# A planner that also schedules the lead-in and searches by replays, and gate rows from split sums, in a one-core DiT layer

## The chip, the cores and the metric

One core of a Trainium2 chip runs the program. The metric is device time in microseconds from start to end of one execution; the time before is the median of three executions on the same chip. The profile is of one further execution. Engines: TensorE (PE, with its weight loads PEld), VectorE (DVE), ScalarE (ACT), GpSimd (POOL), and SyncE (SP), which issues nearly all DMAs.

## The reference

One layer of a diffusion transformer in float32: 256 latent tokens and 256 context tokens of width 2048. The conditioning vector c (and c_ctx for the context) gives six modulation vectors through w_ada; the first two scale and shift the input of a q/k/v projection of width 3072, whose heads go to windowed attention with a sink (A) and to global attention with normalised q and k (B). Then an output projection, a gated residual with layer norm, and a SwiGLU network of hidden width 5632, again with gated residual and layer norm.

```python
sh1, sc1, g1, sh2, sc2, g2 = ada_mods(c, w_ada, b_ada)       # silu(c) @ w_ada + b_ada, split in six
h = modulate(x, sh1, sc1) @ w_in                             # likewise for ctx, with its own mods
x = layer_norm(ALPHA * x + g1 * (heads @ w_out), ln1_g, ln1_b)
u = modulate(x, sh2, sc2)
x = layer_norm(ALPHA * x + g2 * ((silu(u @ w_gate) * (u @ w_up)) @ w_down), ln2_g, ln2_b)
```

## The kernel before, in words

**Products.** A float32 product is three fp32r products (`mm3`, lines 291 to 294): both operands are split into a high half (cast to fp32r on ScalarE) and a low half (the difference, on VectorE), and high x high, low x high and high x low are summed in PSUM. Weights come by DMA as raw tiles of 128 partitions and are split in pieces of 128x1024 (lines 282, 283 and 543, 546).

**The planned part** (to some 400 us) computes the modulation columns, q/k/v, attention and the output projection. The 16 tiles of the contraction of the q/k/v projection are taken in five groups of 1, 1, 2, 4 and 8 (`GROUPS`). For each group, `flow_columns` sums the columns of w_ada for shift and scale on TensorE (line 595), copies the bank (line 629), transposes it by small products with `sel` (line 634) and adds the bias (lines 640, 642). `flow_part` transposes x and ctx (line 699), modulates them and splits the result (lines 710 to 727; a group of one tile goes by line 710 and 712). `flow_blocks` and `flow_block` run the products with six blocks of w_in and empty the accumulators to SBUF (lines 778 to 782): in the first two groups each accumulator receives one triple of products and is then emptied, on VectorE for the second. Then follow attention and `flow_out`. `flow_vector` sums the first gate's columns on VectorE all the while.

**What sets the order.** Each piece of work is a step of `Flow`: an engine, an assumed duration, the steps it comes after, and the buffers it takes and gives back. `forward` simulates a list schedule: whenever an engine is free, it starts the ready step of least rank for which buffers are free. `backward` gives each step the latest start that keeps the end, and these become the ranks of the next round; the best of eight rounds (by its own simulated end) is emitted, and every engine then executes its instructions in that order. Loads are charged by row length (`dma_ns`: 390, 340 or 290 bytes per ns), their landing 2 us later. The begin times per engine say from when the plan may use each.

**The lead-in** is not ordered by the plan: `F.pulls` (at the end of the planned part) takes steps out of the planned order and emits them behind a trigger. The transposes of the first group stand behind the first sum; the casts of the first two w_in pieces and the modulations behind the second addition (the copy of the sums, line 629, therefore before the first cast, line 543); the casts of the third and fourth piece behind accumulators' emptying; the column sums of the second group behind 13 products of the first (`PULL`), those of the third behind four of the second. Warm-up products (`warm`, line 342) stand between the quarters of the second sum and, as steps `WARMS`, behind it.

```python
for _ in range(self.ROUNDS):
    order, last = self.forward()
    if last < end:
        best, end = [(s, s.start, [b.pool for b in s.take]) for s in order], last
    late = self.backward(last)
```

**The rest** (not planned by `Flow`) is w_gate and w_up, then w_down in four column blocks (`down_steps`, `last_steps`). Beside the blocks, VectorE sums the second gate's columns (line 416) in four stretches of 512; `ada_rows` ends each with `rows_from`: one float32 product of a tile of ones with the 128x512 sums (line 426), which sums over the partitions and gives the row to all of them, and a copy to `g2sb` (line 427). The split weights go through four buffers for each half (`HL_BUFS`).

Of the kernel before, what the change touches and what calls it, by code (L numbers as in the profile page):

```python
# [46 lines left out]
WARM = 56  # L47
WARMS = (32, 33, 35, 36, 37, 38)
# [8 lines left out]
PULL = 12  # L57
# [14 lines left out]
class Flow:  # L72
# [8 lines left out]
    ROUNDS = 8  # L81

    def __init__(self, room, begin):
        self.room, self.begin, self.steps, self.at, self.pulls = dict(room), begin, [], 0.0, []
# [96 lines left out]
    def run(self):  # L181
        best, end = None, math.inf
        for _ in range(self.ROUNDS):
            order, last = self.forward()
            if not order:
                break
            if last < end:
                best, end = [(s, s.start, [b.pool for b in s.take]) for s in order], last
# [4 lines left out]
        rooms, then, count, done = {}, {}, {}, set()  # L193
        for s, s.start, pools in best:
            rooms[s] = pools
        for trigger, steps in self.pulls:
            if isinstance(trigger, tuple):
                of, i = trigger
                trigger = [s for s, _, _ in best if s in of][i]
            then.setdefault(trigger, []).extend(steps)  # L200
        held = {s for steps in then.values() for s in steps}

        def emit(s):
            done.add(s)
            for b, b.pool in zip(s.take, rooms[s]):
                pass
            s.fn()
            for n in then.get(s, ()):
                emit(n)

        for s, _, _ in best:
            if s not in held:
                emit(s)
        assert len(done) == len(best), "a pulled step has no trigger"
# [3 lines left out]
def dit_layer(ctx: ExitStack, tc: tile.TileContext, x, c, cx, c_ctx, w_ada, b_ada, w_in, q_norm_g,  # L218
# [125 lines left out]
    wps = Buf("wk")  # L344
    wps.t = wk_bank()[:, :P]
# [114 lines left out]
    def const_tables():  # L460
        nc.gpsimd.tensor_scalar_mul(nsink, sinkb, -1.0)
        for t in range(NT):
            for g, cg, sg in ((gq, cosQ, sinQ), (gk, cosK, sinK)):
# [19 lines left out]
             {"SP": 2100.0, "PE": 3800.0, "ACT": 4300.0, "DVE": 4000.0, "POOL": 4000.0})  # L483
# [12 lines left out]
    F.room["b4"] -= 4  # L496
# [82 lines left out]
    last_load, lead = [], {}  # L579

    def flow_columns(c0, ncol, shift, scale, ats, at):

        width = ncol * P
        n1 = ncol == 1
# [16 lines left out]
        for g in range(ns):  # L601
# [3 lines left out]
            ns1 = nk / 4 * (40 + 1.67 * width)  # L605
            if c0:
# [15 lines left out]
            if g == 0:  # L622
                lead[c0, "both"] = prev
# [19 lines left out]

        a = F.add("ACT", 60 + 0.9 * width, copy, [prev], [sb], [bank])
        b = F.add("PE", 224 * ncol, sums, [a], [ps], [sb])
        adds = [F.add("DVE", 160, lambda i=i: add(i), [b], give=[ps]) for i in range(2)]
        if n1:
            lead[c0, "copy"], lead[c0, "sums"], lead[c0, "adds"] = a, b, adds
# [13 lines left out]
    def flow_part(k0, n, at, each):  # L662
# [5 lines left out]
        def load_x():  # L668
            if k0 == 0:
                return  # L670
# [3 lines left out]
        def load_cx():  # L674
            if k0 == 0:
                cx_room.t = cx0
                return
# [4 lines left out]
        F.at = at + 0.5 * each if k0 else -2.0  # L682
        ns = dma_ns(n * P * SEQ * 4, n * P * 4)
        loads = [F.add("SP", max(ns, 500), load_x), F.add("SP", max(ns, 500), load_cx, take=[cx_room])]
        for s in range(2):
# [3 lines left out]
            for j0 in range(0, n, 2):  # L689
# [13 lines left out]
                def modulate(j, s=s, j0=j0, ps=ps, uf=uf, rooms=rooms):  # L703
# [3 lines left out]
                    if n == 1:  # L707
                        rooms[0].t = b4([P, 4, SEQ], F32R, "uh")
                        rooms[1].t = b4([P, 4, SEQ], F32R, "ul")
                        nc.scalar.activation(rooms[0].t[:, 0, :], ps.t[:, :SEQ], AF.Identity,  # L710
                                             bias=shc[:, k, s : s + 1], scale=scc[:, k, s : s + 1])
                        nc.vector.tensor_scalar(uf.t[:, 0, :], ps.t[:, :SEQ], scc[:, k, s : s + 1], shc[:, k, s : s + 1],
                                                op0=ALU.mult, op1=ALU.add)
                        return
                    nc.scalar.activation(uf.t[:, j, :], ps.t[:, j * SEQ : (j + 1) * SEQ], AF.Identity,
                                         bias=shc[:, k, s : s + 1], scale=scc[:, k, s : s + 1])

                def cast(rooms=rooms, j0=j0, nj=nj, uf=uf):
# [1065 lines left out]
```

## Time and profile before

| what | us |
|---|---|
| median of three executions | 1138.43 (1137.34 to 1139.28) |
| the profiled execution: its own time | 1134.76 |
| its span, first to last instruction | 1133.0 |
| TensorE busy | 1111.8 |
| VectorE busy | 841.2 |
| ScalarE busy | 547.5 |
| GpSimd busy | 39.7 |

The profiled execution's own time holds 1.8 us around the span, and lies 3.67 us under the median. Busy time counts an engine's instructions joined where they overlap; a row's own time is that of the instruction from start to its modelled end, so that products in a row overlap and their starts, not their lengths, tell their pace.

### The profile page before, as it was taken

How to read it: one execution, taken by the hardware profiler on the slowest of the kernel's cores; microseconds unless marked ns; L12 is line 12 of the kernel's file. 1: busy time of each engine (PE TensorE's matmuls, PEld its weight loads, DVE VectorE, ACT ScalarE, POOL GpSimd, SP SyncE). 2: the span in 40 equal slices, each digit the busy share in tenths (PEclk: the TensorE clock that was granted, in tenths of full speed). 3: DMA queues.
4: the chain of work that ended last, by engine and by line, in shares of the span. 5: the costliest groups of instructions: out<-in, count | busy, mean ns of one | idle time of the engine just before them, and what ended most of it. 6: DMA issues, size and time to landing. Idle time of an engine off the chain costs nothing.

```text
span 1133.0 us, 14075 instructions
## 1 busy us (share of the span) xinstructions
PE 1111.8 (98%) x5259; PEld 892.6 (79%) x5259; DVE 841.2 (74%) x1066; ACT 547.5 (48%) x790; POOL 39.7 (4%) x82
## 2 busy tenths in 40 slices
PE   8999999999999999999999999999999999999996
PEld 6666588788887787888888888888888888888884
DVE  4763589999989987877767566767766787676576
ACT  3341464877774365454464444445444344333342
POOL 1000050110100001000000000000000000000000
PEclk9999999999999999999999999999999999999998
DMA  9999999686999689998866766777677889877641
GB/s 306 365 393 396 386 370 370 238 261 200 372 334 391 230 309 343 320 326 307 312 223 217 251 223 224 243 243 255 217 249 243 311 314 328 318 283 245 203 147 74
DMA packets 178317, 321.26 MB, mean 284 GB/s; under 512 B 8732, under 2 KB 43196, under 8 KB 175943
## 3 DMA queue, kind: packets, MB, share of 16 engines
q1 hardware_dynamic: 177528, 320.03, 80.9%
q8 instruction: 41, 0.67, 0.2%
q10 hardware_dynamic: 720, 0.33, 0.1%
q14 instruction: 28, 0.23, 0.1%
HBM read 304.07 MB, written 16.25 MB: 283 GB/s over the span
## 4 chain that ended last, share of the span: by engine, by line
PE 91%; DMA 4%; DVE 2%; ACT 2%; issue 0%; POOL 0%; DVEq 0%; SPq 0%; ACTq 0%; POOLq 0%
PE acc L292 28%; PE acc L294 27%; PE acc L293 27%; PE wk L1025 2%; PE wk L595 2%; DMA raw<-in_w_in_dram 2%; DMA raw<-in_w_ada_dram 1%; DMA pd<-hx 1%; DVE lo L546 1%; PE wk L292 1%; PE wk L294 1%; PE wk L293 1%; DMA raw<-in_w_gate_dram 1%; DVE lo L283 1%; ACT hi L543 0%
## 5 line engine op out<-in xcount | busy, mean ns | idle before, releaser
L283 DVE TENSOR_TENSOR lo<-raw,hi 128x1024 fp32r<-128x1024 f32 x258 | 311.8, 1221 | 173.2 <-ACT hi L282 170.4
L282 ACT CAST hi<-raw 128x1024 fp32r<-128x1024 f32 x258 | 270.6, 1055 | 334.7 <-PE acc L294 296.5
L292 PE MATMUL acc<-hi,u2h 128*128 128x512 f32 x704 | 274.7, 390 | 0.2 <-ACT hi L282 0.2
L293 PE MATMUL acc<-lo,u2h 128*128 128x512 f32 x704 | 274.1, 389 | 0.8 <-DVE lo L283 0.8
L294 PE MATMUL acc<-hi,u2l 128*128 128x512 f32 x704 | 274.0, 389 | 0.0
L293 PEld LDWEIGHTS acc<-lo,u2h 128*128 128x128 f32 x704 | 132.2, 188 | 28.5 <-DVE lo L283 1.1
L292 PEld LDWEIGHTS acc<-hi,u2h 128*128 128x128 f32 x704 | 132.1, 188 | 28.5 <-ACT u2h L1559 0.8
L294 PEld LDWEIGHTS acc<-hi,u2l 128*128 128x128 f32 x704 | 132.1, 188 | 27.9 <-DVE u2l L1560 0.5
L543 ACT CAST hi<-raw 128x1024 fp32r<-128x1024 f32 (+1 forms) x86 | 87.7, 1030 | 107.4 <-DMA raw<-in_w_in_dram 51.3
L292 PE MATMUL acc<-hi,hTh 128*128 128x512 f32 x344 | 135.6, 394 | 0.4 <-ACT acc L1709 0.4
L294 PE MATMUL acc<-hi,hTl 128*128 128x512 f32 x344 | 133.9, 389 | 0.0
L293 PE MATMUL acc<-lo,hTh 128*128 128x512 f32 x344 | 133.9, 389 | 0.0
L416 DVE SCALAR_TENSOR_TENSOR adav<-raw,cs,adav 128x512 f32<-128x512 f32 (+1 forms) x128 | 121.3, 948 | 12.3 <-DMA raw<-in_w_ada_dram 10.3
L546 DVE TENSOR_TENSOR lo<-raw,hi 128x1024 fp32r<-128x1024 f32 (+1 forms) x86 | 101.7, 1193 | 17.3 <-ACT hi L543 17.3
L292 PE MATMUL acc<-hi,uh 128*128 128x512 f32 x256 | 103.1, 403 | 2.6 <-DVE kvacc L782 1.1
L293 PE MATMUL acc<-lo,uh 128*128 128x512 f32 x256 | 100.3, 392 | 2.0 <-DVE lo L546 2.0
L294 PE MATMUL acc<-hi,ul 128*128 128x512 f32 x256 | 100.2, 392 | 0.3 <-DVE ul L727 0.3
L292 PEld LDWEIGHTS acc<-hi,hTh 128*128 128x128 f32 x344 | 64.6, 188 | 15.2 <-issue 1.0
L293 PEld LDWEIGHTS acc<-lo,hTh 128*128 128x128 f32 x344 | 64.6, 188 | 14.3 <-issue 0.7
L294 PEld LDWEIGHTS acc<-hi,hTl 128*128 128x128 f32 x344 | 64.6, 188 | 13.3
L292 PEld LDWEIGHTS acc<-hi,uh 128*128 128x128 f32 x256 | 48.1, 188 | 20.4 <-issue 7.0
L293 PEld LDWEIGHTS acc<-lo,uh 128*128 128x128 f32 x256 | 48.1, 188 | 12.0 <-DVE lo L546 3.0
(219 smaller groups left out, 1137.6 us busy)
## 6 DMA issues: line engine op xcount, KB each, us to landing
raw<-in_w_ada_dram SPq DMA_DIRECT2D x70, 1024.0 KB, 7.0
raw<-in_w_gate_dram SPq DMA_DIRECT2D x44, 1024.0 KB, 5.2
raw<-in_w_up_dram SPq DMA_DIRECT2D x44, 1024.0 KB, 5.1
raw<-in_w_down_dram SPq DMA_DIRECT2D x44, 1024.0 KB, 4.9
raw<-in_w_ada_dram SPq DMA_DIRECT2D x48, 512.0 KB, 5.2
raw<-in_w_in_dram SPq DMA_DIRECT2D x18, 1024.0 KB, 7.0
raw<-in_w_out_dram SPq DMA_DIRECT2D x16, 1024.0 KB, 8.0
pd<-hx SPq DMA_DIRECT2D x64, 128.0 KB, 4.1
```

The source lines that it names most:

```text
L282: nc.scalar.copy(hi[:, :n], raw[:, s : s + n])
L283: nc.vector.tensor_tensor(lo[:, :n], raw[:, s : s + n], hi[:, :n].bitcast(F32), op=ALU.subtract)
L292: nc.tensor.matmul(ps, lhsT=xh, rhs=w[0], start=first, stop=False, skip_group_check=seeded)
L293: nc.tensor.matmul(ps, lhsT=xh, rhs=w[1], start=False, stop=False, skip_group_check=seeded)
L294: nc.tensor.matmul(ps, lhsT=xl, rhs=w[0], start=False, stop=last, skip_group_check=seeded)
L416: nc.vector.scalar_tensor_tensor(a[:, c : c + piece], raw[:, f : f + piece], cs[:, 4 * (g * (G4 * NB // w) + j) + 2, None], a[:, c : c + p ...
L543: nc.scalar.copy(hl.hi[:, :n], raw.t[:, s : s + n])
L546: nc.vector.tensor_tensor(hl.lo[:, :n], raw.t[:, s : s + n], hl.hi[:, :n].bitcast(F32), op=ALU.subtract)
L595: nc.tensor.matmul(bank.t[32 * j : 32 * j + 32, :width], lhsT=cs[:, 4 * k + 2 - 2 * i : 4 * k + 34 - 2 * i], rhs=raw.t[:, c * width : (c + ...
L1025: nc.tensor.matmul(o_ps.t[:, : 2 * P].rearrange("p (g q) -> p g q", q=32), lhsT=v, rhs=pv[:, k], start=k == 0, stop=k == 3)
```

## The change

`Flow.run` no longer moves steps by `pulls`. A new `search` makes eight rounds of `forward` and `backward` with noise on the ranks, then 800 moves, each of which shifts the ranks of a random part of the steps and makes a new forward schedule. A schedule is judged by `replay`: it runs the order through in-order engines with buffers used first in, first out, once by the assumed durations and four times with each duration varied by 3%, and the mean end decides. The lead-in's steps are ordered by this plan like the rest; they have new durations and begin times, the small w_in pieces are charged to the b4 buffers in which they stand, and the first group's transposes come after the first column sum. The `warm` products between quarters are left out; two stand behind the second sum and four behind the small products with `sel`. For the second gate's rows, the sums are split in halves and multiplied by an fp32r tile of ones: a cast on ScalarE, a difference on VectorE and two fp32r products.

```diff
-WARM = 56
-WARMS = (32, 33, 35, 36, 37, 38)
-PULL = 12
...
+    SEED, SIGMA, MOVES, DRAWS, JITTER = 312, 600.0, 800, 4, 0.03
...
+    def replay(self, order, draws):
+
+        index = {s: i for i, s in enumerate(order)}
+        gives, left = {}, {}
...
+        free, plan = {p: [None] * n for p, n in self.room.items()}, []
+        for s in order:
+            deps = [(index[a], self.lag(a, s) - early) for a, early in s.after]
+            for b in s.take:
+                if not free[b.pool]:
+                    return math.inf
+                old = free[b.pool].pop(0)
+                for g in gives.get(old, ()):
+                    deps.append((index[g], self.AGAIN if b.pool.endswith("raw") else self.OTHER[g.eng]))
...
+            plan.append((s.eng, s.ns, deps))
+        total = 0.0
+        for draw in draws:
+            busy, ends = dict(self.begin), []
+            for (eng, ns, deps), f in zip(plan, draw):
+                t = busy[eng]
+                for i, lag in deps:
+                    if ends[i] + lag > t:
+                        t = ends[i] + lag
+                busy[eng] = t + ns * f
+                ends.append(busy[eng])
+            total += max(ends)
+        return total / len(draws)
...
+    def search(self):
+        rng = random.Random(self.SEED)
+        draws = [[1.0] * len(self.steps)]
+        draws += [[max(0.8, rng.gauss(1.0, self.JITTER)) for _ in self.steps] for _ in range(self.DRAWS)]
...
             for i, s in enumerate(self.steps):
-                s.rank = (late[s], i)
+                s.rank = (late[s] + rng.gauss(0.0, sigma), i)
...
+        for _ in range(self.MOVES):
+            sigma, share = rng.choice((100.0, 300.0, 1000.0)), rng.choice((0.01, 0.03, 0.1, 0.3))
+            for r, s in zip(base, self.steps):
+                s.rank = (r[0] + (rng.gauss(0.0, sigma) if rng.random() < share else 0.0),) + r[1:]
...
+            order, last = self.forward()
+            if not order or last > score + 1000:
+                continue
+            mean = self.replay(order, draws)
+            if mean <= score:
+                best, score, base = self.keep(order), mean, ranks
+        return best, score
...
+    def split_rows(sb, dst, s):
+        hi = whl.tile([P, SUB * NB], F32R, tag="hi", name="hi")[:, :NB]
+        lo = whl.tile([P, SUB * NB], F32R, tag="lo", name="lo")[:, :NB]
+        split(hi, lo, sb[:, s : s + NB])
+        ps = wk_bank()
+        nc.tensor.matmul(ps, lhsT=onesr, rhs=hi, start=True, stop=False)
+        nc.tensor.matmul(ps, lhsT=onesr, rhs=lo, start=False, stop=True)
+        nc.scalar.copy(dst[:, s : s + NB], ps)
...
     def ada_rows(c0, dst, sums):
         def done(sb):
             for s in range(0, dst.shape[-1], NB):
-                rows_from(sb, dst, s)()
+                split_rows(sb, dst, s)
...
-             {"SP": 2100.0, "PE": 3800.0, "ACT": 4300.0, "DVE": 4000.0, "POOL": 4000.0})
+             {"SP": 1800.0, "PE": 6300.0, "ACT": 5100.0, "DVE": 4200.0, "POOL": 4000.0})
+    F.room["wk"] -= 1
...
-                prev = F.add("PE", 2 * ns1 + 420, both, [l0, l1, prev], [bank] if g == 0 else [], [r0, r1])
+                prev = F.add("PE", 1860, both, [l0, l1, prev], [bank] if g == 0 else [], [r0, r1])
             else:
-                def quarters(i, r):
-                    for q in range(4):
-                        fn(0, i, r, 4 * q, 4 * q + 4)
-                        if i and 0 < q < 3:
-                            warm(wps.t, 1)
-
-                prev = F.add("PE", ns1, lambda r=r0: quarters(0, r), [l0, prev], [bank] if g == 0 else [], [r0])
-                lead["sum"] = prev
-                prev = F.add("PE", ns1, lambda r=r1: quarters(1, r), [l1, prev], [], [r1])
+                def one(i, r):
+                    fn(0, i, r, 0, nk)
+                    if i:
+                        warm(wps.t, 2)
+
+                prev = F.add("PE", 1080, lambda r=r0: one(0, r), [l0, prev], [bank], [r0])
+                first_sum.append(prev)
+                prev = F.add("PE", 1520, lambda r=r1: one(1, r), [l1, prev], [], [r1])
...
+            if c0 == 0:
+                warm(wps.t, 4)
...
-        loads = [F.add("SP", max(ns, 500), load_x), F.add("SP", max(ns, 500), load_cx, take=[cx_room])]
+        if k0:
+            loads = [F.add("SP", max(ns, 500), load_x), F.add("SP", max(ns, 500), load_cx, take=[cx_room])]
+        else:
+            loads = first_sum * 2
+            cx_room.pool, cx_room.t = "b4", cx0
...
+                if n == 1:
+                    a = F.add("ACT", 520, high, [p] + ready, rooms)
+                    b = F.add("DVE", 470, whole, [a], [uf], [ps])
+                    b = F.add("DVE", 360, rest, [b], give=[uf])
+                    u[k0, s][1].append((a, b))
+                    continue
...
-                piece, = flow_weights(w_in, k0, 1, b0 * NB, m * NB, where, small=k0 == 0)
-                if k0 == 0:
-                    lead["w", i] = piece[1]
+                piece, = flow_weights(w_in, k0, 1, b0 * NB, m * NB, where if k0 else ("b4",), small=k0 == 0)
...
-            v = F.add("PE", 1800, values, g, [o_ps], [pT, *kv_room[w]])
+            v = F.add("PE", 1540, values, g, [o_ps], [pT, *kv_room[w]])
...
-    T = 18.0
+    T = 12.0
...
-    F.pulls.append((lead["sum"], [flip0, flip1]))
-    F.pulls.append((lead[0, "adds"][1], [w0, mod0, l0, rest0, mod1, rest1, w1, l1]))
-    for i in (2, 3):
-        F.pulls.append((lead["evacs"][2 * i - 3], list(lead["w", i])))
...
-    F.pulls.append(((made, PULL), [lead[P, "both"]]))
...
+    onesr = pb.tile([P, P], F32R, tag="onesr", name="onesr")
+    nc.scalar.copy(onesr, ones)
```

## Rows read from the trace of the kernel before

**Rows 1.** The page: the span, and the chain that ended last by engine.
```profile
span 1133.0 us, 14075 instructions
...
PE 91%; DMA 4%; DVE 2%; ACT 2%; issue 0%; POOL 0%; DVEq 0%; SPq 0%; ACTq 0%; POOLq 0%
```

**Rows 2.** By stretch (us): its length, engines busy (instructions), granted clock, DMA share, GB/s.
```profile
0.00:20.00 20.00, 16.62 (x133) 12.72 (x133) 8.85 (x14) 7.13 (x12) 3.48 (x9) 1.00 0.94 291
...
13.29:20.00 6.71, 5.45 (x22) 3.86 (x21) 5.79 (x9) 3.98 (x6) 0.00 (x0) 1.00 1.05 307
20.00:30.00 10.00, 9.50 (x98) 7.42 (x99) 5.63 (x12) 3.35 (x7) 0.00 (x0) 1.00 1.03 335
30.00:43.00 13.00, 11.21 (x92) 6.65 (x92) 10.41 (x17) 3.58 (x6) 0.00 (x0) 1.00 0.97 333
43.00:80.00 37.00, 37.00 (x208) 25.48 (x208) 24.09 (x37) 12.16 (x16) 0.00 (x0) 1.00 1.04 395
80.00:150.00 70.00, 68.67 (x385) 46.64 (x384) 34.93 (x47) 30.06 (x50) 0.00 (x0) 1.00 1.03 387
150.00:300.00 150.00, 150.00 (x696) 122.34 (x695) 140.95 (x237) 102.01 (x219) 27.66 (x54) 1.00 0.84 293
300.00:350.00 50.00, 48.18 (x208) 38.76 (x207) 45.61 (x61) 36.83 (x66) 0.00 (x0) 1.00 1.00 351
350.00:400.00 50.00, 49.90 (x252) 38.92 (x250) 44.43 (x76) 19.02 (x30) 1.60 (x5) 1.00 0.83 305
...
860.00:1100.00 240.00, 240.00 (x1053) 197.27 (x1052) 170.31 (x178) 94.78 (x95) 1.58 (x3) 1.00 0.77 272
...
1100.00:1133.00 33.00, 21.69 (x95) 17.30 (x93) 22.67 (x37) 10.49 (x27) 0.00 (x0) 0.88 0.17 64
```

**Rows 3.** TensorE's waits, 6 to 400 us: total us, times, longest us.
```profile
PE acc L293 <- DVE lo L546: 2.0, 3, 0.8
PE acc L294 <- DVE oTl L1037: 1.8, 1, 1.8
PE acc L292 <- DVE kvacc L782: 1.1, 2, 0.8
PE wk L595 <- DMA raw<-in_w_ada_dram: 0.6, 1, 0.6
```

**Rows 4.** The lead-in in order of time: start us, length us, instruction [idle before it].
```profile
9.95 0.49 PE L342 MATMUL wk<-ident 128*128 128x128 f32 x2
...
11.67 0.27 ACT L629 COPY ada<-wk 128x128 f32<-128x128 f32 x1 [2.19 <-PE wk L595]
11.84 0.62 ACT L543 CAST hi<-raw 128x512 fp32r<-128x512 f32 x1
...
13.29 0.50 PE L292 MATMUL acc<-hi,uh 128*128 128x512 f32 x1
...
13.73 0.68 DVE L546 TENSOR_TENSOR lo<-raw,hi 128x512 fp32r<-128x512 f32 x1
...
14.47 0.51 PE L293 MATMUL acc<-lo,uh 128*128 128x512 f32 x1 [0.67 <-DVE lo L546]
...
25.08 1.95 PE L595 MATMUL wk<-raw,cs 128*32 128x128 f32 x64
```

**Rows 5.** The first gate row of the last stage, in order of time.
```profile
904.31 1.06 ACT L282 CAST hi<-raw 128x1024 fp32r<-128x1024 f32 x1 [3.02 <-PE acc L294]
...
905.25 0.40 PE L294 MATMUL acc<-hi,hTl 128*128 128x512 f32 x1
...
905.48 1.02 PE L426 MATMUL wk<-adav,ones 128*128 128x512 f32 x2
...
906.54 0.59 ACT L427 COPY g2sb<-wk 128x512 f32<-128x512 f32 x1 [1.17 <-PE wk L426]
...
906.58 0.39 PE L293 MATMUL acc<-lo,hTh 128*128 128x512 f32 x1
...
907.02 1.05 ACT L282 CAST hi<-raw 128x1024 fp32r<-128x1024 f32 x1
```

More of the change, by code (lines that the diff above doesn't have):

```diff
@@ L179, in backward, with keep @@
         return start
-    def run(self):
-        best, end = None, math.inf
+    def replay(self, order, draws):
+        index = {s: i for i, s in enumerate(order)}
+        gives, left = {}, {}
+        for s in order:
+            for b in s.give:
+                gives.setdefault(b, []).append(s)
+                left[b] = left.get(b, 0) + 1
+        free, plan = {p: [None] * n for p, n in self.room.items()}, []
+        for s in order:
+            deps = [(index[a], self.lag(a, s) - early) for a, early in s.after]
[5 more added lines that the diff above has]
+                    deps.append((index[g], self.AGAIN if b.pool.endswith("raw") else self.OTHER[g.eng]))
+            for b in s.give:
+                left[b] -= 1
+                if left[b] == 0:
+                    free[b.pool].append(b)
+            plan.append((s.eng, s.ns, deps))
[11 more added lines that the diff above has]
+        return total / len(draws)
+    def keep(self, order):
+        return [(s, s.start, [b.pool for b in s.take]) for s in order]
+    def search(self):
+        rng = random.Random(self.SEED)
+        draws = [[1.0] * len(self.steps)]
+        draws += [[max(0.8, rng.gauss(1.0, self.JITTER)) for _ in self.steps] for _ in range(self.DRAWS)]
+        best, score, sigma = None, math.inf, self.SIGMA
         for _ in range(self.ROUNDS):
+            ranks = [s.rank for s in self.steps]
             order, last = self.forward()
@@ L186, in run @@
                 break
-            if last < end:
-                best, end = [(s, s.start, [b.pool for b in s.take]) for s in order], last
+            mean = self.replay(order, draws)
+            if mean < score:
+                best, score, base = self.keep(order), mean, ranks
             late = self.backward(last)
             for i, s in enumerate(self.steps):
-                s.rank = (late[s], i)
+                s.rank = (late[s] + rng.gauss(0.0, sigma), i)
+            sigma *= 0.8
         assert best, "no step can start"
[L193 to L205, printed above, removed]
+        for _ in range(self.MOVES):
+            sigma, share = rng.choice((100.0, 300.0, 1000.0)), rng.choice((0.01, 0.03, 0.1, 0.3))
+            for r, s in zip(base, self.steps):
+                s.rank = (r[0] + (rng.gauss(0.0, sigma) if rng.random() < share else 0.0),) + r[1:]
+            ranks = [s.rank for s in self.steps]
+            order, last = self.forward()
+            if not order or last > score + 1000:
+                continue
+            mean = self.replay(order, draws)
+            if mean <= score:
+                best, score, base = self.keep(order), mean, ranks
+        return best, score
+    def run(self):
+        for s, s.start, pools in self.search()[0]:
+            for b, b.pool in zip(s.take, pools):
                 pass
             s.fn()
[L208 to L214, printed above, removed]
 @with_exitstack
@@ L642, in add @@
                 nc.vector.scalar_tensor_tensor(scale, pv[:, :, 1, :], 1.0, bc, op0=ALU.add, op1=ALU.add)
[L644 to L648, printed above, removed]
+        a = F.add("ACT", 60 + 0.82 * width, copy, [prev], [sb], [bank])
+        b = F.add("PE", 217 * ncol - 70 if c0 else 1150, sums, [a], [ps], [sb] if c0 else [sb, wps])
+        adds = [F.add("DVE", 160, lambda i=i: add(i), [(b, 0 if c0 else 1000)], give=[ps]) for i in range(2)]
         return a, adds
@@ L767, in flow_block @@
                                         done + len(cols) == ng, ends.get(r))
-                lead.setdefault(("products", k0), []).append(ends[r])
                 for m in rooms:
@@ L1406, in dit_layer @@
     a = F.add("DVE", 3300, lambda: scalars(0), [(outs[n, 0], 80) for n in range(4)])
-    (flip0, mod0, rest0), (flip1, mod1, rest1) = (lead[0, s] for s in range(2))
-    (w0, l0), (w1, l1) = (lead["w", i] for i in range(2))
-    F.pulls.append((lead["sum"], [flip0, flip1]))
-    F.pulls.append((lead[0, "adds"][1], [w0, mod0, l0, rest0, mod1, rest1, w1, l1]))
-    for i in (2, 3):
-        F.pulls.append((lead["evacs"][2 * i - 3], list(lead["w", i])))
-    (flip0, mod0, rest0), (flip1, mod1, rest1) = (lead[P, s] for s in range(2))
-    made = lead["products", 0]
-    F.pulls.append(((lead["products", 1], 3), [lead[2 * P, "both"]]))
-    F.pulls.append(((made, PULL), [lead[P, "both"]]))
-    F.pulls.append(((made, PULL), [lead[P, "copy"]]))
-    F.pulls.append(((made, PULL + 1), [lead[P, "sums"], *lead[P, "adds"]]))
-    F.pulls.append(((made, PULL + 2), [flip0, flip1, mod0, rest0, mod1, rest1]))
     zroom = [Buf("wk"), Buf("wk")]
```

53 lines of the change are left out of this document (17 added, 36 removed).

## The prediction

> **What bounds the kernel now.** I read the page first: one chain, and 91% of it is TensorE [rows 1]. So time is gained only where TensorE stands still or where its own work shrinks. Next the table by stretch [rows 2], to see where it stands still: from 860 to 1100 us it is busy 240.00 of 240.00, and it is full from 43 to 80 and from 150 to 300. What is left inside the planned part (from the first product at 13.29 us [rows 4] to about 400 us) is 1.26 + 0.50 + 1.79 us between 13.29 and 43, 1.33 between 80 and 150, 1.82 between 300 and 350 and 0.10 after that: 6.8 us. The list of waits [rows 3] says whom TensorE waited for: VectorE nearly always (the low halves of w_in, the emptying of the accumulators, once 1.8 us for oTl), and a load only once, 0.6 us, in the lead-in. The lead-in in order of time [rows 4] shows what one wait costs. L292 starts at 13.29 and L293 at 14.47, 1.18 us later. Products that follow each other start 0.23 us apart (L294 at 905.25, the next at 905.48 [rows 5]). So 0.95 us is lost where the list puts 0.67: a wait costs about 0.28 us more than its idle time, since the matmuls no longer overlap. The waits number seven between 13.29 and 43 us and four after (those of 0.6 us and less in all, but for the load, are not shown): the lead-in loses 3.55 + 7 x 0.28 = 5.5 us, the rest of the plan 3.25 + 4 x 0.28 = 4.4. **Nothing that reorders the plan can return more than 9.9 us.**
>
> **The change, part by part.**
>
> *The search.* It adds no instruction. It gives another order on all five queues up to about 400 us, scored with in-order queues, first-in-first-out buffers and 3% noise on the durations. Its gain lies between the 9.9 us above and a loss that the trace bounds only by its like: the longest wait of TensorE there is 1.8 us, 2.1 with the filling [rows 3], and two new ones of that size would cost 4.2. I take a third of the 9.9. In the lead-in that is 1.8 of 5.5: VectorE is busy 10.41 of 13 us from 30 to 43 and the transfers fill their engines (share 0.94 to 1.05) [rows 2], so order can move work there but make no room. In the rest it is 1.4 of 4.4, most of it from the oTl wait, which is an order on VectorE and no lack of its time. A third and not all, because a plan by average durations has already been followed here and these waits are what was left between plan and chip; the same gap will open elsewhere.
>
> *The lead-in as steps.* The pulls go: transposes after the first sum, the first w_in pieces and modulations after the second addition, the next group's column sums behind 13 products (at 25.08 us [rows 4]). The same instructions are issued, now where the planned start puts them, their loads on SP too. What is new is the order on ScalarE. Before, the copy of the first sums (11.67) comes ahead of the cast of the first w_in piece (11.84, 0.62 us) [rows 4]. The new durations put the landing of that piece at 1.8 + 2 x 3.6 + 0.7 + 2.0 = 11.7 and the end of the second sum at about 12.5, so I expect the cast first. If the piece lands as late as 11.84, the copy and all behind it wait until 12.46: up to 0.8 us later, with the sums on TensorE, the two additions, the modulations and the first product behind them. In exchange the low half (0.68 us on VectorE) can be made before the additions, and the 0.95 us of the second product goes. Ends: 0.8 lost, 0.95 gained; I take nothing, near the middle, and keep 0.9 each way for the range.
>
> *The warm-up products.* Two calls between the quarters of the second sum go, the six after it stay as two and four. The two ran while the next quarter was on its way (0.49 us at 9.95, two records) [rows 4], so they cost nothing and their going returns nothing. The cover is that wait; gone, it would be 2 x 0.2 us gained. A loss would come by the clock: the granted clock is 1.00 (2.4 GHz) in every stretch to 1100 us and 0.88 on average in the last one, after TensorE has stopped [rows 2]. A quarter's eight to sixteen products still run between any two waits, so I put nothing.
>
> *The pools.* The small w_in pieces are now charged to the b4 buffers in which they stand and no longer to raw buffers, so loads may be planned earlier. The transfers are full to 150 us [rows 2]; earlier issue only lengthens the queue. Nothing.
>
> *The last stage's gate rows.* Four times the fp32 product with ones becomes a cast, a subtraction and two fp32r products. Now: L426 starts at 905.48 and the second product after it at 906.58 [rows 5], 1.10 us, of which one product is 0.23; so 0.87. Then: 2 x 0.23 = 0.46. Gain 0.41 x 4 = 1.6 us, on the path, since TensorE has no gap there [rows 2]. Added beside it: on ScalarE 0.62 us and on VectorE 0.68 us, four times (the same shapes in [rows 4]); these engines are busy 95 and 170 of 240 us [rows 2]. The wait that it adds: the two products stand behind cast and subtraction, and these behind the sums on VectorE; behind them on TensorE stands the next step of w_down. The pair of operands also takes one of four buffers, so one later cast starts a half step later. In [rows 5] the cast at 907.02 starts 1.65 us after the one before it has ended (904.31 + 1.06), held up by the copy at 906.54, and TensorE had no wait; that much delay is covered. If the cover is gone it is a wait like that of the first product, 0.95 x 4 = 3.8 us lost. I take the gain: the row says that the cover is there. The copy of ones once: 0.2 us on ScalarE, beside products.
>
> **Sum.** 1.8 + 1.4 + 1.6 = 4.8 us off the profiled execution's own 1134.76 us: 1129.96. That execution was 3.67 us under the median of the three runs (1138.43); against the median it is 1133.6.
>
> **A rule against it.** The transfers moved 395 GB/s from 43 to 80 us [rows 2]. The Trainium skill, DMA: Bandwidth & Descriptors, section Bandwidth, has loads from HBM bound at about 358 GB/s per core; by that the plan's 390 for long rows would be out of reach, its lead-in would starve, and the lead-in's 1.8 us would not be there (sum 3.0). The trace goes past that figure, so I keep the sum; the case itself is weighed as rival B.
>
> **The rivals.**
>
> *A. Most of the waits go.* Two thirds of 9.9 us, plus 1.6: 8.2 off, 1130.2. For it: the waits are those of order on VectorE, which is idle in between. The data would be there: up to group 2's first product the kernel needs w_ada for four rows of tiles (8.4 MB), w_in for two (3.1), x and context (1.0) and a first half megabyte, 13.1 MB; by 43 us it had moved 5.8 + 3.35 + 4.3 = 13.5 [rows 2]. Against it: that leaves nearly no slack. 0.17.
>
> *B. Order gives nothing.* The transfers and VectorE pace the lead-in, and what one wait gives back the next takes. Only the last stage remains: 1.6 off, 1136.8. For it: shares of 0.97 to 1.05 to 43 us [rows 2]. This is also the case in which the change doesn't do what it says. 0.20.
>
> *C. Slower: TensorE waits for loads in the lead-in.* In the queue of TensorE a column sum now stands where the plan expects its data, no longer behind products that were counted by hand. The plan charges 390, 340 or 290 GB/s by row length, some 365 for the mix; from 20 to 43 us the trace moved 335 and 333 [rows 2], 7.7 MB, so a plan by those rates, 21.1 us where the trace took 23.0, is 1.9 us early. Each column sum that is reached so blocks the ready products behind it: 1.9 + 0.28 = 2.2 us, twice (for groups 2 and 3) 4.4, less 1.6: 2.8 slower, 1141.2. It decides once such waits pass the 4.8 us of the sum. Against it: before, TensorE waited for a load only 0.6 us [rows 3]. 0.17.
>
> **The numbers.** About 0.2%, 2.3 us, is what a measurement of this kernel can tell from no change. The forecast, a third of the waits and the last stage, has 0.46, its own range 1131.5 to 1135.8 (the 0.9 us of the order on ScalarE and half of the third either way). With A faster is 0.63, B makes 0.20 for the same, C 0.17 for slower. The range from 1128.5 to 1141 takes in A and most of C.
>
> **What would show it.** Right: between 13 and 43 us under 3 us of idle TensorE; no wait on oTl over 1 us; in the last stage two products of ones 0.23 us apart with no idle before them; the cast at about 11.7 ahead of the copy. Wrong: TensorE waiting for w_ada after 20 us (C); the first product after 14.1 us; a granted clock under 1.00 before 1100 us; a wait of L293 just behind a gate row (the buffer); unchanged idle time up to 400 us (B).

## The result, and the profile after

Beside 20 runs of the kernel before (median 1135.80 us, 1132.21 to 1139.49) the changed kernel took 1140.14 us (20 runs, 1135.29 to 1144.66): a ratio of 1.0034, 95% interval [1.0021, 1.0047]. It is slower by 4.3 us at the medians. The forecast of 1133.6 was set against 1138.43 us; the ratio makes 1142.3 of that, above the upper end of the range (the median of 1140.14 itself lies inside it). The profiled executions are 1134.76 us (span 1133.0) and 1137.55 us (span 1135.8).

The page of the kernel after: its span, and the chain that ended last by engine.

```profile
span 1135.8 us, 14062 instructions
...
PE 93%; DVE 3%; ACT 1%; DMA 1%; issue 0%; ACTq 0%; SPq 0%; DVEq 0%
```

Against [rows 1], 1% of the chain is DMA where 4% was. How far the two kernels have come can be read from one tile after the other. The view by tile, first products of each weight with the high half of an operand (count, shortest, median and longest in ns, then the first and the last start in us); first the kernel before:

```profile
L292 PE MATMUL acc<-hi,uh x256: 387/389/582, 13.3 to 254.1; 128*128 128x512 f32 x128
L292 PE MATMUL acc<-hi,oTh x128: 389/389/792, 254.7 to 387.3; 128*128 128x512 f32 x128
L292 PE MATMUL acc<-hi,u2h x704: 389/389/502, 392.1 to 877.6; 128*128 128x512 f32 x176
L292 PE MATMUL acc<-hi,hTh x344: 389/389/798, 878.3 to 1118.5; 128*128 128x512 f32 x172
```

and the kernel after:

```profile
L331 PE MATMUL acc<-hi,uh x256: 389/389/796, 16.1 to 260.0; 128*128 128x512 f32 x128
L331 PE MATMUL acc<-hi,oTh x128: 389/389/798, 257.9 to 390.0; 128*128 128x512 f32 x128
L331 PE MATMUL acc<-hi,u2h x704: 389/389/501, 396.4 to 882.2; 128*128 128x512 f32 x176
L331 PE MATMUL acc<-hi,hTh x344: 389/389/499, 882.9 to 1121.5; 128*128 128x512 f32 x172
```

The first product is 2.8 us late, the last of the planned part (oTh) 2.7, the first after the handover to the second half (u2h) 4.3, the first of w_down (hTh) 4.6 and its last 3.0. So the last stage gained 1.6 us, as forecast, and of the 4.6 us that the kernel is behind at the first hTh product 4.3 were lost before 400 us. The table by stretch of the kernel after (length, engines busy with their instructions in the order PE, PEld, DVE, ACT, POOL, granted clock, DMA share, GB/s), against [rows 2]:

```profile
10.00:20.00 10.00, 6.08 (x41) 4.05 (x38) 5.83 (x11) 4.32 (x7) 0.00 (x0) 0.79 1.09 356
16.06:22.50 6.44, 5.63 (x12) 3.97 (x13) 4.98 (x9) 1.02 (x2) 0.00 (x0) 0.50 1.08 340
20.00:30.00 10.00, 10.00 (x95) 7.98 (x94) 6.17 (x9) 3.89 (x7) 0.00 (x0) 0.87 0.83 275
30.00:43.00 13.00, 13.00 (x84) 9.80 (x83) 10.16 (x19) 3.44 (x6) 0.00 (x0) 1.00 1.03 367
...
80.00:150.00 70.00, 70.00 (x388) 47.23 (x387) 34.51 (x46) 27.16 (x42) 0.00 (x0) 1.00 1.02 385
...
200.00:300.00 100.00, 96.93 (x449) 76.12 (x447) 92.60 (x181) 76.29 (x182) 14.32 (x38) 1.00 0.78 261
300.00:350.00 50.00, 50.00 (x219) 40.91 (x218) 46.89 (x64) 37.66 (x67) 0.00 (x0) 1.00 0.99 348
350.00:400.00 50.00, 48.62 (x239) 37.82 (x238) 45.15 (x73) 18.40 (x27) 1.08 (x4) 1.00 0.89 329
400.00:440.00 40.00, 38.05 (x184) 31.00 (x183) 35.76 (x49) 24.50 (x38) 2.46 (x5) 1.00 0.82 286
860.00:1100.00 240.00, 240.00 (x1060) 198.61 (x1059) 174.02 (x185) 98.66 (x101) 1.58 (x3) 1.00 0.78 276
```

and three stretches of the kernel before that [rows 2] do not have:

```profile
10.00:20.00 10.00, 8.73 (x59) 6.36 (x55) 6.03 (x11) 5.38 (x9) 0.00 (x0) 1.00 1.04 335
...
200.00:300.00 100.00, 100.00 (x475) 80.94 (x474) 94.08 (x186) 78.89 (x189) 13.38 (x38) 1.00 0.77 253
400.00:440.00 40.00, 39.07 (x181) 31.70 (x182) 35.98 (x44) 22.99 (x32) 3.80 (x5) 1.00 0.84 302
```

The search did what it was made for where it could see: the 0.50 + 1.79 + 1.33 us of idle TensorE between 20 and 150 us are gone, and so are the 1.82 between 300 and 350. But TensorE now stands still for 3.92 us from 10 to 20 (1.27 before), 3.07 from 200 to 300 (none before), 1.38 from 350 to 400 (0.10) and 1.95 from 400 to 440 (0.93). And from the first product to 22.5 us it ran at a granted clock of 0.50 (1.2 GHz): the 5.63 us that it was busy there are work of some 2.8 us at full speed (an estimate: half of them). Its waits, 6 to 400 us, against [rows 3]:

```profile
PE wk L679 <- ACT ada L674: 1.4, 1, 1.4
PE acc L331 <- ACT u2h L1580: 1.4, 1, 1.4
PE wk L644 <- DMA raw<-in_w_ada_dram: 1.3, 3, 0.6
PE acc L333 <- DVE oTl L1080: 1.1, 2, 0.6
PE acc L332 <- DVE lo L596: 1.0, 1, 1.0
PE acc L331 <- ACT uh L757: 1.0, 1, 1.0
PE acc L333 <- DVE ul L772: 0.8, 1, 0.8
```

and one more at 402.7 us, from the same view of 400 to 460 us:

```profile
PE wk L1432 <- DVE xt L1215: 1.9, 1, 1.9
```

The oTl wait of 1.8 us is down to 0.6. New are a chain by ScalarE (ada, uh) and VectorE (ul) in the lead-in, and two waits at the handover (u2h, xt). The lead-in in order of time, against [rows 4]:

```profile
11.20 0.43 PE L644 MATMUL wk<-raw,cs 128*32 128x128 f32 x8 [0.32 <-DMA raw<-in_w_ada_dram]
11.56 0.71 PE L381 MATMUL wk<-ident 128*128 128x128 f32 x4
12.39 1.04 ACT L593 CAST hi<-raw 128x1024 fp32r<-128x1024 f32 x1 [2.86 <-DMA raw<-in_w_in_dram]
13.34 0.26 ACT L674 COPY ada<-wk 128x128 f32<-128x128 f32 x1
...
13.50 0.62 ACT L593 CAST hi<-raw 128x512 fp32r<-128x512 f32 x1
13.66 0.39 PE L679 MATMUL wk<-sel,ada 128*128 128x4 f32 x2 [1.39 <-ACT ada L674]
13.90 1.14 PE L381 MATMUL wk<-ident 128*128 128x128 f32 x8
14.49 1.05 ACT L593 CAST hi<-raw 128x1024 fp32r<-128x1024 f32 x1 [0.38 <-DMA raw<-in_w_in_dram]
...
15.45 1.02 ACT L757 ACTIVATE uh<-wk,shc,scc 128x256 fp32r<-128x256 f32 x2
16.06 0.80 PE L331 MATMUL acc<-hi,uh 128*128 128x512 f32 x1 [1.02 <-ACT uh L757]
```

The first sums end at 11.63, but ScalarE has stood 2.86 us in front of the cast of a w_in piece that lands at 12.39; the copy of the sums queues behind it (13.34; before 11.67), and two more casts stand ahead of the modulation (15.45).

### The profile page after: what moved, and what is told of

The parts are those of the page before. It is cut to its first block, busy times and chain, and to the rows that moved or that the text cites. A ratio compares the mean times of both kernels' runs of the same rounds, so it can differ in the third digit from the quotient of the medians.

```text
span 1135.8 us, 14062 instructions
## 1 busy us (share of the span) xinstructions
PE 1112.2 (98%) x5255; PEld 893.2 (79%) x5255; DVE 844.4 (74%) x1070; ACT 551.4 (49%) x795; POOL 41.6 (4%) x82
## 4 chain that ended last, share of the span: by engine, by line
PE 93%; DVE 3%; ACT 1%; DMA 1%; issue 0%; ACTq 0%; SPq 0%; DVEq 0%
PE acc L331 28%; PE acc L333 28%; PE acc L332 28%; PE wk L644 2%; PE wk L1068 2%; PE wk L743 1%; PE wk L331 1%; DVE hx L1050 1%; PE wk L333 1%; PE wk L332 1%; DMA raw<-in_w_in_dram 1%; DMA cxt<-in_ctx_dram 0%; DVE lo L596 0%; PE wk L1401 0%; PE wk L475 0%
## 5 line engine op out<-in xcount | busy, mean ns | idle before, releaser
L333 PEld LDWEIGHTS acc<-hi,ul 128*128 128x128 f32 x256 | 48.6, 190 | 12.3 <-DVE ul L772 1.7
```

What stands on the lines that cost most here:

```text
L333: nc.tensor.matmul(ps, lhsT=xl, rhs=w[0], start=False, stop=last, skip_group_check=seeded)
```

## The experiments

Eleven kernels ran, each beside the kernel before. The clock is the mean over the executions of a kernel of the granted TensorE clock that each run lists (to three places); time x clock is the mean of the products, an estimate of what the kernel would take had the clock always been full. The estimate is rough: the last stretch, at 0.88 over 33 us in [rows 2] with TensorE busy for 21.69 of them, lowers every mean, and warm_more, which has the plan of after, comes out 1.7 us above after. The row of before belongs to the runs beside rows_only, lead_order, warm_more and flips_first; beside the others the median of before was 1135.43 to 1135.80, and each ratio is taken against its own.

| kernel | us, median (runs) | ratio to before, 95% | clock | time x clock |
|---|---|---|---|---|
| before | 1134.99 (35) | 1 | 0.9964 | 1131.4 |
| after | 1140.14 (20) | 1.0034 [1.0021, 1.0047] | 0.9922 | 1130.9 |
| rows_only | 1132.93 (12) | 0.9977 [0.9961, 0.9993] | 0.9968 | 1129.6 |
| lead_order | 1138.63 (12) | 1.0023 [1.0006, 1.0040] | 0.9942 | 1131.8 |
| warm_more | 1137.58 (12) | 1.0019 [1.0004, 1.0034] | 0.9954 | 1132.6 |
| flips_first | 1137.04 (12) | 1.0019 [1.0004, 1.0033] | 0.9933 | 1130.0 |
| both | 1135.63 (12) | 1.0001 [0.9989, 1.0013] | 0.9954 | 1130.5 |
| both_late | 1134.96 (12) | 0.9991 [0.9980, 1.0003] | 0.9963 | 1130.7 |
| values_1800 | 1135.44 (12) | 0.9999 [0.9986, 1.0011] | 0.9938 | 1128.4 |
| seed_4 | 1143.49 (6) | 1.0064 [1.0047, 1.0082] | 0.9917 | 1133.6 |
| val_lead | 1133.10 (12) | 0.9980 [0.9970, 0.9990] | 0.9968 | 1129.6 |
| val_sum2 | 1134.04 (12) | 0.9987 [0.9971, 1.0003] | 0.9955 | 1129.1 |
| val_sum2_warm | 1131.10 (6) | 0.9960 [0.9946, 0.9973] | 0.9973 | 1128.3 |

**rows_only**, the kernel before with the gate rows alone:

```
-                rows_from(sb, dst, s)()
+                split_rows(sb, dst, s)
+    onesr = pb.tile([P, P], F32R, tag="onesr", name="onesr")
+    nc.scalar.copy(onesr, ones)
```

> The kernel before with the split gate rows of the last stage alone; its plan and lead-in are untouched. Theory 1 (the parts are independent): 0.4 us for each of four rows, 1.6 us faster than before, ratio about 0.9986, and no wait of TensorE on either product of ones. Rival (the split takes a buffer that the next casts need): a wait of L293 behind a row, up to 0.95 us each, ratio 1.000 to 1.002.

0.9977, faster than both kernels. The first product of each of its four rows, in the view by tile, and then the first row in order of time in the kernel after:

```profile
L428 PE MATMUL wk<-hi,onesr x4: 389/389/389, 905.1 to 1053.5; 128*128 128x512 f32 x4
```

```profile
904.18 0.69 DVE L328 TENSOR_TENSOR lo<-adav,hi 128x512 fp32r<-128x512 f32 x1 [1.56 <-ACT hi L327]
...
910.08 0.39 PE L468 MATMUL wk<-hi,onesr 128*128 128x512 f32 x1
910.31 0.39 PE L469 MATMUL wk<-lo,onesr 128*128 128x512 f32 x1
```

The two products start 0.23 us apart and find their operands 5 us old: the added cast and subtraction are covered. This part of the change is right and worth the 0.2% alone; the loss is in the rest.

**lead_order**, the plan of after with the lead-in's instructions issued in the order of before (copy, sums and additions, narrow cast, modulations; the wide cast after them), and the two first small loads of w_in changed over:

```
-        for s, s.start, pools in self.search()[0]:
+        for s, s.start, pools in lead_order(self.search()[0]):
...
+    chunk = [copy, sums, *adds, c1, h0, w0, r1, u0, h1, w1, u1, c0, r0]
```

> The changed kernel; the same plan, but in the lead-in the copy of the first sums, the additions and the modulations are emitted ahead of the casts of all but one small w_in piece, and the two first small loads change places, as in the kernel before. Theory 1 (what the lead-in loses stays lost, since TensorE is full from 20 to 200 us): first product at 13.3 us instead of 16.1, granted clock 1.00 throughout, 3 to 4 us faster than the changed kernel, ratio to before 1.000 to 1.001. Rival (the loads set the pace to 150 us): first product early as well, but TensorE waits for loads or for VectorE before 100 us and the end moves by under 1 us, ratio 1.003.

```profile
11.65 0.27 ACT L674 COPY ada<-wk 128x128 f32<-128x128 f32 x1 [2.16 <-PE wk L644]
...
12.65 1.02 ACT L757 ACTIVATE uh<-wk,shc,scc 128x256 fp32r<-128x256 f32 x2 [0.22 <-DVE shc L687]
...
13.27 0.49 PE L331 MATMUL acc<-hi,uh 128*128 128x512 f32 x1
```

With the same warming products the first product comes at 13.27: the 2.8 us are the order of the lead-in. How much of it is ScalarE's order, and how much that of the two loads and of VectorE, which changed with it, this run does not separate. The granted clock was 1.00 from 10 to 30 us. Yet the ratio fell only to 1.0023. In the profiled execution the clock fell elsewhere, at the handover:

```profile
400.00:410.00 10.00, 8.77 (x31) 7.32 (x32) 6.24 (x13) 3.85 (x8) 0.95 (x1) 0.66 0.42 146
```

**warm_more**, after with more warming products in the lead-in's waits and the order untouched:

```
-                        warm(wps.t, 2)
+                        warm(wps.t, 9)
...
-                warm(wps.t, 4)
+                warm(wps.t, 10)
```

> The changed kernel with 9 in place of 2 warm-up products behind the second sum and 10 in place of 4 behind the small products; the plan and every other order are the same. Theory 1 (the granted clock fell because TensorE had little to do from 11.5 to 16 us): the clock stays at 1.00, the first product stays at 16.1 us, the products from 16 to 22.7 us follow each other 0.23 us apart instead of 0.43, up to 3 us are gained by 25 us and about 2 at the end, ratio 1.0015. Rival (VectorE, which empties one accumulator per product there, or the loads hold the pace at either clock): clock 1.00, but waits of TensorE between 17 and 33 us take the gain back, ratio 1.003.

The first product stays late (15.88 us in the profiled execution), but the clock does not fall in the lead-in; it fell once in the attention:

```profile
10.00:20.00 10.00, 8.42 (x68) 7.11 (x69) 5.78 (x11) 4.31 (x7) 0.00 (x0) 1.00 1.09 358
...
235.00:245.00 10.00, 8.98 (x35) 6.70 (x36) 8.56 (x16) 6.46 (x24) 0.00 (x0) 0.83 0.70 234
```

The mean clock went from 0.9922 to 0.9954 and the median 2.6 us down (by the ratios 0.0015, 1.7 us; the two intervals overlap). So the clock costs time of its own, apart from the order.

**flips_first**, after with the transposes of the second half (L1432) ahead of the column sums (L1401) on TensorE, as before had them; **both**, this and lead_order; **both_late**, both with the scale sums merged one step later, so that they stand no longer inside the second layer-norm chain on VectorE:

```
-    run(merge(first_half[3 : 2 * ONE_F], scales))
+    run(first_half[3:4])
+    run(merge(first_half[4 : 2 * ONE_F], scales))
```

> The changed kernel; the same plan, but the two transposes for the next stage (L1432) are emitted on TensorE ahead of the column sums of L1401, as they stood before, and nothing else moves. Theory 1 (the handover loses because the chain from the transposes over ScalarE and VectorE to the next products is no longer hidden beside the sums): the waits of 1.4 us at 396 and 1.9 us at 402 go, about 3 us, of which the wait on the low half some 40 us later, which the kernel before had and the changed one has not, takes back up to 1.5; net 1.5 to 3 us faster than the changed kernel, ratio to before 1.001 to 1.002. Rival (VectorE is late there for other reasons, so the chain ends when it did): one wait in place of two, under 1 us gained, ratio 1.003.

> The changed kernel with the lead-in's order of lead_order and the handover's order of flips_first, nothing else. Theory 1 (both losses are separate, and each costs its wait plus the stretch at half clock that follows it in some executions): the gains add, 1.2 and 1.7 us off the changed kernel's 3.9, ratio to before 1.0005 to 1.0015, mean granted clock 0.995 or more instead of 0.992. Rival (the time is lost by the plan as a whole and comes back elsewhere): ratio stays at 1.002 or above, clock under 0.995.

> As both, and the sums of the next w_ada stretch (L456 at the handover) are merged from one step of w_gate and w_up later on, so that on VectorE they no longer stand inside the second layer-norm chain. Theory 1 (the second wait of the handover, 2.0 us at 402 us, is an order on VectorE): that wait falls under 0.5 us, the clock stays up there, 1.5 to 2.5 us faster than both, ratio 0.999 to 1.000. Rival (the later sums are late for the products after them, as the low half was in the kernel before): a new wait of 1 to 2 us between 430 and 500 us, no gain on both.

flips_first halves the first wait of the handover (u2h, 1.4 to 0.7 us) and leaves the second (xt, 1.9); both is level with before, 1.0001; both_late takes the second wait out of the list and has another one at 434 us in its place, the 0.8 us that before had there too (its view of the waits, 6 to 460 us):

```profile
PE acc L332 <- DVE lo L322: 0.8, 1, 0.8
PE acc L331 <- ACT u2h L1580: 0.7, 1, 0.7
```

The traces show these waits shrink or go; from one of the three kernels to the next the intervals overlap, so what each step at the handover is worth is read from traces alone: TensorE's idle time from 380 to 440 us is 3.33 us in after and 2.63 in flips_first, 2.63 in both and 1.79 in both_late.

**values_1800**, after with one duration of the plan changed:

```
-            v = F.add("PE", 1540, values, g, [o_ps], [pT, *kv_room[w]])
+            v = F.add("PE", 1800, values, g, [o_ps], [pT, *kv_room[w]])
```

> The changed kernel, but the plan charges 1800 instead of 1540 ns for the four products of probabilities and values; the plan found is another one, with the same lead-in. Theory 1 (1540 is the time from the first to the next start and leaves out that the next products then start 0.19 us late; with it the plan takes waits of 3 us at 230 us into account that fall on a busy chip, 4.4 us in all from 217 to 298): TensorE's waits from 210 to 300 us fall under 1 us, ratio 1.000 to 1.002. Rival (any new plan brings its own waits): those go, others of 2 us or more come between 20 and 400 us, ratio 1.003 or above.

1800 is what the kernel before had. Level with before (0.9999), though its lead-in is as late as that of after (first product at 16.00, clock 0.78 from 10 to 20 us). It is another plan throughout (the transposes of the handover stand ahead of the sums in it, and its wait on xt is 0.3 us); the largest thing that went is the attention's idle time, 3.07 us to 0.48:

```profile
200.00:300.00 100.00, 99.52 (x469) 79.29 (x468) 93.71 (x185) 77.88 (x187) 14.24 (x38) 1.00 0.80 255
```

One plan could have this by chance, but the others agree: from 200 to 300 us TensorE stands still for 4.00 us in seed_4, planned with 1540, and for 0.05 in val_sum2, planned with 1800 (both below). In the trace of after, what follows such a step starts 1.73 us behind it (241.50 to 243.23), or 1.54 us behind it (252.38 to 253.92) and is then some 0.2 us slow to its own next start (0.41 us for 0.23). So 1540 is some 0.2 us short.

**seed_4**, after with another seed of the search (312 to 4), whose plan the planner itself judged worse:

> The changed kernel with seed 4 instead of 312 for the search: another plan, whose judged end by the replays is 388.9 us where that of seed 312 is 384.5. Its lead-in puts the copy of the sums before the long casts, its rest has more waits by the plan's own durations. Theory A (the replays judge truly): 4.4 us slower than the changed kernel, ratio 1.007. Theory B (the judge doesn't know the clock, what follows the plan's end, nor that greedy starts are taken; plans that differ by 4 us in it do not differ so on the chip): ratio 1.004 or less, with the first product before 15 us and no fall of the clock in the lead-in.

1.0064, the slowest of all, 3.4 us over after: of this pair, the replays rank the plans as the chip does; one pair does not show that they always do. Its lead-in is a second reading of the order on ScalarE. A cast stands ahead of the copy here too, but the narrow piece is loaded first, and its cast (0.62 us) starts at 11.72 in its trace. The copy, at 12.25, is 0.58 us later than before and the first product, at 13.86, 0.57; the clock stays at 1.00 from 10 to 30 us. Its attention by stretch:

```profile
200.00:300.00 100.00, 96.00 (x447) 76.36 (x446) 90.90 (x179) 76.27 (x184) 11.11 (x38) 0.98 0.74 244
```

**val_lead**, values_1800 with the order of lead_order:

> The plan made with 1800 for the product of probabilities and values, and the lead-in in the order of the run lead_order. If the late lead-in is the rest of the loss, the first product starts near 13.3 us as in lead_order (16.0 in values_1800), the granted clock stays at full speed from 10 to 30 us, the 400th product is 2 to 3 us earlier than in values_1800, and the ratio to the kernel before is 0.997 to 0.998 (values_1800 gave 0.9999; 2.4 us of 1135 are 0.0021). If the search's rearrangement is worth nothing beyond the gate rows, it is no better than rows_only, 0.9977. If a fall of the clock elsewhere takes the place of the one in the lead-in, it stays at 0.999 to 1.000.

0.9980, as expected from the lead-in's share; the first product at 12.98, the clock at 1.00 from 10 to 30, and 0.27 us of idle time from 200 to 300. It is no better than rows_only (0.9977): with the lead-in in the old order, nothing that the search rearranged shows beyond the gate rows.

**val_sum2** and **val_sum2_warm**, the planner alone with two durations nearer to the trace, without and with the warming products of warm_more:

```
-                prev = F.add("PE", 1520, lambda r=r1: one(1, r), [l1, prev], [], [r1])
+                prev = F.add("PE", 560, lambda r=r1: one(1, r), [l1, prev], [], [r1])
-            v = F.add("PE", 1540, values, g, [o_ps], [pT, *kv_room[w]])
+            v = F.add("PE", 1800, values, g, [o_ps], [pT, *kv_room[w]])
```

> The planner alone, with two durations nearer to the trace: 1800 for the product of probabilities and values in place of 1540, and 560 in place of 1520 for the second step of the first column sums; no order by hand. If the wrong durations alone put the wide cast ahead of the copy of the sums, the plan now puts the copy first: copy at about 11.7 us, first product at 13.3 to 15.5, clock at full speed in the lead-in, ratio 0.997 to 0.999. If the planner cannot see what matters (a free engine that ought to wait for a more urgent step, a judged end that stops short of the handover), the loss moves to other places of the plan and the ratio stays at 1.000 or above.

> The run val_sum2 with 9 and 10 warming products in the lead-in in place of 2 and 4 (as in warm_more); nothing of the order differs. If the granted clock of the lead-in is what val_sum2 still loses (mean granted clock of its executions 0.9955 against 0.9968 in rows_only and val_lead), the clock stays at full speed from 10 to 30 us, the mean of the executions comes to 0.9965 or more, and the ratio goes from 0.9987 to about 0.9975. If the warming products hold up the column sums, or the clock falls in another stretch instead, the ratio stays at 0.9985 or above.

With 560 the plan itself puts the copy first. Two lines of val_sum2 in order of time, and its lead-in and attention by stretch:

```profile
11.14 0.27 ACT L674 COPY ada<-wk 128x128 f32<-128x128 f32 x1 [2.15 <-PE wk L644]
...
13.92 1.01 ACT L757 ACTIVATE uh<-wk,shc,scc 128x256 fp32r<-128x256 f32 x2
```

```profile
10.00:20.00 10.00, 7.12 (x42) 5.20 (x37) 5.37 (x10) 4.15 (x7) 0.00 (x0) 0.83 1.09 358
...
200.00:300.00 100.00, 99.95 (x473) 80.20 (x472) 94.02 (x184) 78.81 (x188) 10.82 (x38) 1.00 0.77 256
```

The modulation still queues behind wide casts (13.92; in lead_order 12.65), so the first product comes at 14.53 and the clock still falls. The warming products keep it at 1.00 and bring the mean to 0.9973. They are not free here: the small products with `sel` come at 13.53 us (11.55 in val_sum2) and the first product at 15.90, 1.4 us later, and the kernel is still the faster one:

```profile
10.00:20.00 10.00, 9.37 (x71) 7.62 (x72) 6.02 (x12) 4.89 (x8) 0.00 (x0) 1.00 1.10 366
```

val_sum2_warm, four numbers away from after, is the fastest of all: 1131.10 us, 0.9960 [0.9946, 0.9973]. It beats both kernels; its interval overlaps that of rows_only, and just meets that of val_sum2. Whether more warming products would speed up the kernel before or rows_only too was not run, so it is not shown that the search has a part in the step from 0.9977 to 0.9960.

## Why the prediction was wrong

**The last stage's gate rows: right.** 1.6 us were forecast, 1.6 came (+4.6 at the first hTh product, +3.0 at the last), with TensorE at 240.00 of 240.00 us and no wait behind a gate row.

**The lead-in's order on ScalarE: the step that failed.** I read the order right (cast ahead of copy) and wrote "Ends: 0.8 lost, 0.95 gained; I take nothing". The copy came 1.67 us later and the first product 2.77. The bound took the length and the landing of the piece from [rows 4] (0.62 us, 11.84). For a narrow piece that comes first the bound holds: in seed_4 the first product is 0.57 us late. In the order of after the first piece is the wide one, 1.04 us long and there at 12.39, and I looked at the first place in ScalarE's queue only: two more casts stand ahead of the modulation, and on VectorE 1.23 + 2.05 us of low halves ahead of ul. lead_order undid it, and the first product came 2.79 us earlier. val_sum2 shows where the order of cast and copy comes from. By the plan's 1520 the second sum ends at about 12.5, as I had worked it out; in the trace it ended at 11.63. So the cast looked due before the copy: the three plans made with 1520 (after, values_1800, seed_4) put a cast first, and with 560 the plan turns them round. What is left then (the modulation behind a wide cast) has to do with how the planner fills time: a free engine takes the next ready step and is not kept for one that is due a moment later. That is read from its code, and val_sum2's 14.53 against val_lead's 12.98 agrees with it.

**The warm-ups and the clock: failed too, and by an estimate the dearest.** "A quarter's eight to sixteen products still run between any two waits, so I put nothing." From 11.63 to 16.06 us TensorE ran 0.71 + 0.39 + 1.14 us and stood still for the rest, and from there to 22.5 us it was granted 0.50. Over all executions the clock is 0.0042 lower; as a share of 1138 us that is 4.8 us, as much as the whole loss of 4.3. That is an estimate: in warm_more, where the clock rose by 0.0032 (3.6 us by the same working), 1.7 to 2.6 us came back. The low mean is more than the lead-in's fall alone, since executions show falls at other new waits too (235 to 245 us in warm_more, 400 to 410 in lead_order). warm_more and val_sum2_warm raised the clock with nothing changed but the warming products, and the medians fell by 2.6 and 2.9 us (the ratios by 0.0015 and 0.0027, with intervals that overlap in both pairs).

**The waits of the plan: a third forecast, nothing left.** In the column time x clock after stands 0.5 us under before, where the gate rows alone stand 1.8 under (rows_only). The column is too rough for the plan's own loss, but of the 3.2 us that were to be gained it shows nothing. That was not for lack of gain: 3.62 us of idle time between 20 and 150 and most of the oTl wait went, nearer to rival A than to my third, and not only because TensorE ran slowly there: lead_order, at full clock from 10 to 30 us, has 0.46 us left from 20 to 43 and none from 80 to 150. It was given back in the lead-in (above), in the attention (3.07 us, by values_1800, seed_4 and val_sum2 a wrong duration: 1540 for a step that holds TensorE longer) and at the handover, which lies behind the end that the planner judges. I had written that "the same gap will open elsewhere" and that two new waits could cost 4.2 us; I did not make them a rival.

**The rivals.** C had the sign, not the mechanism: TensorE waited for w_ada 1.3 us, all of it before 11.7 us, and from 20 to 43 it was full. B's "order gives nothing" is near the net of the plan, for reasons that it did not name. Of the signs that I listed, two that meant "wrong" were there: a first product after 14.1 us and a granted clock under 1.00 before 1100. The forecast's own range does not come out of its terms either: 0.9 us and half of the third (1.6) make 1131.1 to 1136.1, not 1131.5 to 1135.8.

## What to carry to other kernels

A planner's durations are inputs like any other: with one that is some 0.2 us short in a step that comes 16 times, the plans had 3 to 4 us of idle TensorE in the attention, and with one that is 1 us long in the lead-in they put a cast ahead of a more urgent copy. Check each against the trace before the search is judged. When an order changes, follow the whole queue of each engine up to the first product, with the sizes of the pieces in the new order, not only the pair that changes places. And where TensorE is the bound, list what it does in each new wait: in warm_more, warming products that left the wait as long as it was brought back 1.7 to 2.6 us by the granted clock alone.

## What the hardware showed that was not expected

The granted clock fell to half for some microseconds after waits of 1 to 2 us: 0.50 from 16.06 to 22.5 us in after, 0.66 on average from 400 to 410 in lead_order, 0.83 from 235 to 245 in warm_more. Not every such wait is followed by a fall: the kernel before has its oTl wait of 1.8 us, and after its own two at the handover (1.4 and 1.9 us), with the clock at 1.00. What tells the one from the other stays open. The Trainium skill, TensorE: Matmul & The Clock Gate, section HAM oscillation — how this bites in real kernels, tells of a kernel whose short runs of matmuls between waits for loads start at the lower clock again and again; the lead-in of after agrees with it in kind (0.50 from its first product on), and shows that the waits need not be for loads: the two longest there, 1.4 and 1.0 us, are for ScalarE. Where the clock falls differs between executions of like plans, and an execution's time goes with its mean clock: those of before took 1138.1 us at 0.995, 1135.9 at 0.996 and 1134.4 at 0.997 (means of 4, 13 and 13). A difference of 0.2% can thus lie between executions of one kernel and go with the clock, and the list of waits of a single profile does not show it.
